# Down projections by seven products, added from PSUM to the residual, with the norm factor in the operands

## The chip, the cores and the metric

The kernel runs on one core of one Trainium2 chip. Its time is the device time of one execution in microseconds: 2298.66 us, the median of three runs (2298.14 to 2299.22).

## The reference

Two macaron layers over 528 tokens (512 plus 16 meta tokens) of width 1024. Each layer is a half-weighted SwiGLU, a mixer (gated linear attention and grouped-query attention, merged by sigmoid gates) and a second half-weighted SwiGLU. Each has an RMS norm ahead, and one stands at the end.

```python
def rmsnorm(x, g):
    y = xf * lax.rsqrt(jnp.mean(xf * xf, axis=-1, keepdims=True) + EPS)
    return (y * g.astype(jnp.float32)).astype(x.dtype)

def swiglu(x, w_gate, w_up, w_down):
    return (jax.nn.silu(x @ w_gate) * (x @ w_up)) @ w_down
...
        h = h + 0.5 * swiglu(rmsnorm(h, norm_gains[l, 0]),
                             ffn_w_gate[l, 0], ffn_w_up[l, 0], ffn_w_down[l, 0])
        h = h + mixer(rmsnorm(h, norm_gains[l, 1]), ...)
        h = h + 0.5 * swiglu(rmsnorm(h, norm_gains[l, 2]), ...)
```

The width of gate and up is 2816, 22 tiles of 128. Everything is float32.

## The kernel before

Activations lie with features on partitions and tokens along the free dimension: the residual `hall` is 8 chunks of 128 features by 528 tokens, and a token half is 264 columns (256 once the meta tokens have been dropped, in the last FFN). A float32 product is made from three matmuls: each operand is split into a rounded high part (`S.copy`, ScalarE, L222 for weights) and the rest (`V.tensor_tensor` subtract, VectorE, L227), and high x high, high x low and low x high are summed in PSUM.

Gate and up run by Strassen's scheme in Winograd's form. Two chunks of input features and two tiles of output features, with two token halves, make 2 x 2 blocks, and seven products stand for eight. `product_of_pair` (L489 to L530, matmuls at L502) does one product of one pair of output tiles: 24 matmuls of 264 columns. Products 1, 6, 7 and 4 add up in one PSUM tile X; snapshots of it on the way are copied out (`snapshot`, L505). Products 1, 2 and 4 use a plain block of weights; 7, 6, 5 and 3 use sums of blocks, which `sums` (L180) has made by DMA: a negated copy on ScalarE (L173), then DMAs that add while they write, issued from GpSimd's queue (L178). `pair` (L422) makes the seven activation blocks of two chunks.

Down runs plainly: `down` (L544) takes 22 hidden tiles to 8 output tiles, with the accumulations of three groups (4, 4 and 3 pairs) added to the residual (`add_to_h`, L471). The norm factor (one number per token) is not in the operands: it is multiplied in after the matmuls, by `scaled` (L467), on gate, on up, on down's output and on the mixer's projections, so that matmuls can start on a chunk before the mean over all chunks is known. `rs` (L458) makes the mean with an all-1/1024 matmul (L388), then Ln, Exp(-0.5) and a Newton step.

The order of weights is a list (`weight_plan`), written by `ffn_steps`. `Weights.use` keeps four blocks of 128 x 1024 made ahead (`AHEAD_MADE`) and six fetched; there are 3 raw buffers, 4 high, 4 low, and 3 and 2 for sums. Plain loads go through SP's queue (L168, L203), adding ones through GpSimd's, a few constants through ScalarE's. Each engine runs its instructions in one fixed order; the tile framework makes that order from the program's order, its priorities and its own estimate of times, and blocks marked `high_priority` come earlier. In the mixer, 12 of a layer's low parts are made by DMA (`by_dma`, L223).

## Time and profile before

| what | us |
|---|---|
| median of three runs | 2298.66 |
| span of the profiled execution, first to last instruction | 2289.1 |
| median less span: what lies around it (the page gives no other time of its own execution) | 9.6 |
| TensorE, matmuls busy | 2225.1 (97%) |
| VectorE busy | 1491.3 (65%) |
| ScalarE busy | 1214.4 (53%) |
| GpSimd busy | 195.1 (9%) |
| matmuls | 16548 |
| DMA, mean | 143 GB/s, 327.79 MB |

Rows of engines give busy time and share of the span. Matmuls are pipelined, so a mean of a group (285 ns at L502) is the latency of one and not its pace; the pace is a stretch of the chain divided by its count. The four FFNs lie at about 8 to 390, 806 to 1163, 1170 to 1536 and 1929 to 2272 us, the mixers between the first and second and the third and fourth.

### The profile page before, as it was taken

The numbers are of one execution on the slowest core, as the hardware profiler recorded it, in microseconds if no ns is written. First come the engines' busy times: TensorE is split into PE (matmuls) and PEld (weight loads), VectorE is DVE, ScalarE is ACT, GpSimd is POOL, SyncE is SP. The second block draws the span as 40 slices with busy tenths as digits, with TensorE's granted clock in tenths as the row PEclk, the third lists the DMA queues.
The fourth block names the chain that finished last, engine by engine and source line by source line (L and its number), as shares of the span: only waits on it lengthen the run. The fifth ranks groups of instructions, "written<-read, shape, count | busy, mean of one in ns | idle before, by whom it ended". The sixth has DMA issues, their size and how long they took to land.

```text
span 2289.1 us, 39919 instructions
## 1 busy us (share of the span) xinstructions
PE 2225.1 (97%) x16548; PEld 2108.4 (92%) x16548; DVE 1491.3 (65%) x2355; ACT 1214.4 (53%) x1785; POOL 195.1 (9%) x218
## 2 busy tenths in 40 slices
PE   5999999999999999999989999999999999999997
PEld 5999999989999999999989999998788888989896
DVE  6656567476775676565676565674768667756566
ACT  7536355344786564453565353553448946636452
POOL 1111010010000010101011110100000001101010
PEclk9999999999999999999989999999999999999999
DMA  8858562211325485766667585632113356859661
GB/s 225 236 150 224 142 175 93 74 57 56 84 56 157 117 214 153 189 180 173 181 141 202 151 219 146 170 98 74 56 65 93 74 156 152 223 149 223 159 176 61
DMA packets 91869, 327.79 MB, mean 143 GB/s; under 512 B 10214, under 2 KB 12646, under 8 KB 91688
## 3 DMA queue, kind: packets, MB, share of 16 engines
q1 hardware_dynamic: 61136, 218.26, 28.7%
q0 software_dynamic: 28800, 104.87, 25.6%
q8 instruction: 130, 2.13, 0.4%
q10 hardware_dynamic: 1752, 2.11, 0.3%
q14 instruction: 51, 0.42, 0.1%
HBM read 264.38 MB, written 2.10 MB: 116 GB/s over the span
## 4 chain that ended last, share of the span: by engine, by line
PE 89%; DVE 5%; DMA 2%; ACT 2%; issue 1%; SPq 0%; DVEq 0%; POOL 0%; ACTq 0%
PE ss L502 36%; PE ss L382 27%; PE mm L382 14%; PE sm L382 3%; PE sm L861 1%; PE sm L878 1%; DVE wlo L227 1%; PE sm L879 1%; PE ss L836 1%; DMA w<-win 1%; PE ss L837 1%; PE ss L388 1%; DMA s<-win 1%; PE ss L718 1%; DMA w<-s 1%
## 5 line engine op out<-in xcount | busy, mean ns | idle before, releaser
L502 PE MATMUL ss<-xc,whi 128*128 128x264 f32 (+1 forms) x4928 | 902.3, 285 | 26.5 <-ACT snap L508 9.7
L502 PEld LDWEIGHTS ss<-xc,whi 128*128 128x128 f32 x4928 | 766.8, 189 | 29.3 <-ACT snap L508 10.3
L502 PE MATMUL ss<-xc,wlo 128*128 128x264 f32 (+1 forms) x2464 | 702.1, 285 | 4.3 <-DVE wlo L227 4.3
L382 PE MATMUL ss<-g,whi 128*128 128x264 f32 (+2 forms) x2668 | 494.2, 301 | 0.0
L502 PEld LDWEIGHTS ss<-xc,wlo 128*128 128x128 f32 x2464 | 466.0, 189 | 5.3 <-DVE wlo L227 5.1
L382 PEld LDWEIGHTS ss<-g,whi 128*128 128x128 f32 x2668 | 388.6, 188 | 17.4
L382 PE MATMUL mm<-x,whi 128*128 128x264 f32 (+1 forms) x1712 | 383.5, 315 | 0.0
L222 ACT CAST whi<-w 128x1024 fp32r<-128x1024 f32 (+1 forms) x221 | 230.8, 1047 | 263.1 <-PE ss L382 118.7
L222 ACT CAST whi<-raw 128x1024 fp32r<-128x1024 f32 x190 | 199.3, 1049 | 299.5 <-PE mm L382 106.9
L227 DVE TENSOR_TENSOR wlo<-w,whi 128x1024 fp32r<-128x1024 f32 (+1 forms) x221 | 267.9, 1218 | 110.7 <-ACT whi L222 108.4
L382 PE MATMUL ss<-g,wlo 128*128 128x264 f32 (+2 forms) x1334 | 309.9, 301 | 0.0
L382 PEld LDWEIGHTS mm<-x,whi 128*128 128x128 f32 x1712 | 279.5, 189 | 18.8 <-issue 2.1
L382 PE MATMUL mm<-x,wlo 128*128 128x264 f32 (+1 forms) x856 | 267.2, 317 | 0.0
L227 DVE TENSOR_TENSOR wlo<-raw,whi 128x1024 fp32r<-128x1024 f32 x166 | 203.1, 1224 | 95.2 <-ACT whi L222 94.2
L382 PEld LDWEIGHTS ss<-g,wlo 128*128 128x128 f32 x1334 | 213.4, 188 | 8.7
L227 DVE TENSOR_TENSOR wlo<-s,whi 128x1024 fp32r<-128x1024 f32 x88 | 107.6, 1223 | 102.0 <-ACT whi L222 101.9
L222 ACT CAST whi<-s 128x1024 fp32r<-128x1024 f32 x88 | 92.4, 1050 | 153.6 <-PE ss L502 135.4
L382 PEld LDWEIGHTS mm<-x,wlo 128*128 128x128 f32 x856 | 160.4, 189 | 10.8 <-issue 2.2
L469 DVE SCALAR_TENSOR_TENSOR t<-ss,rs 128x528 f32<-128x528 f32 (+1 forms) x95 | 66.0, 700 | 127.8 <-PE ss L382 127.7
L173 ACT ACTIVATE s<-w 128x1024 f32<-128x1024 f32 x88 | 93.3, 1060 | 79.2 <-DMA w<-win 41.5
L178 POOL DMA_DIRECT2D s<-win x44 | 40.8, 927 | 497.0 <-ACT s L173 489.2
L508 ACT COPY snap<-ss 128x528 f32<-128x528 f32 (+1 forms) x132 | 77.2, 585 | 0.0
(235 smaller groups left out, 2660.3 us busy)
## 6 DMA issues: line engine op xcount, KB each, us to landing
w<-win SPq DMA_DIRECT2D x219, 512.0 KB, 4.7
raw<-wts SPq DMA_DIRECT2D x190, 512.0 KB, 3.4
s<-win POOLq DMA_DIRECT2D x44, 512.0 KB, 6.8
w<-s POOLq DMA_DIRECT2D x44, 512.0 KB, 5.5
w<-win POOLq DMA_DIRECT2D x44, 512.0 KB, 7.1
s<-w POOLq DMA_DIRECT2D x44, 512.0 KB, 7.4
wlo<-raw POOLq DMA_DIRECT2D x24, 512.0 KB, 4.4
h<-xt SPq DMA_DIRECT2D x3, 528.0 KB, 7.1
```

The lines of the kernel that those rows point to most:

```text
L173: self.nc.scalar.activation(t, w, AF.Copy, scale=-1.0)
L178: self.nc.gpsimd.dma_start(t, src, accum_op=ALU.add)
L222: nc.scalar.copy(hi[:, cs], w[:, cs])
L227: nc.vector.tensor_tensor(lo[:, cs], w[:, cs], hi[:, cs].bitcast(F32), ALU.subtract)
L382: TE.matmul(acc.half[i][:width], lhs, rhs[:, acc.spans[i]], start=first, stop=last)
L388: TE.matmul(a, weights, x[:, hs], start=True, stop=True)
L469: V.scalar_tensor_tensor(cut(dst[rows]), pv[rows], -0.5 * f, cut(rs[rows]), ALU.mult, ALU.mult)
L502: TE.matmul(acc[:, j], a[:, j, k], b[:, at], start=bool(begin and k == 0 and i == 0), stop=k == len(x) - 1 and i == 2, skip_group_check=no ...
L508: S.copy(st[name], acc)
L718: TE.matmul(ats[:n, hh, d * n : (d + 1) * n], prods[d][1][rows, bs], prods[d][0][rows, bs], start=True, stop=True)
L836: TE.matmul(s[:n, i, :HF], lhs, kh[:, hs], start=True, stop=False)
L837: TE.matmul(s[:n, i, :HF], lhs, kl[:, hs], start=False, stop=True)
```

## The change

The down projections are also done by seven products. Their 2 x 2 blocks are the two tiles of a pair of hidden features, two output chunks (m and m + 2, in each half `d` of four chunks) and the two token halves. An FFN is now a list of units: `("U", p)` for a pair of gate and up, `("D", g, d)` for one half of the output over group g; the groups are 3, 2, 3 and 3 pairs. Each product of a D unit has 6 matmuls of 264 columns per pair. Its PSUM tile is added to the residual as it is, by one VectorE operation (`of_half`), so X with products 1, 1+6, 1+6+7 and 1+6+7+4 goes to the places that need it. The hidden activations are made in seven blocks (`of_pair`); the half weight of the FFN goes into the gate. Down's weights come from a new array `wdn` in blocks of 768 or 512 columns, and pass through `sums` like gate's.

The norm factor is multiplied into the operands, by token halves: `square` and `square_chunk` sum squares per half as chunks are finished, `finish(i)` makes the mean and factor of half i and calls `operands(i)`. Products 1 and 2 need only half 0, 5 and 6 need half 1, and `rest` makes what 7, 3 and 4 need. An FFN therefore opens with products 1 and 2 of units 0 and 1 and product 2 of unit 2. Before it, w_out does its last three chunks by halves; the mixer does its first three projections by halves. Projections are copied out without a factor, `by_dma` is gone, and the constants of the mixer are loaded at the start of each mixer. At the end of the kernel each half of the residual is multiplied by its factor in two operations and stored in two DMAs.

```diff
-GROUPS = (4, 4, 3)
-HELD = 4
-PLACE = {p: i for i, p in enumerate("1256743")}
+GROUPS = (3, 2, 3, 3)
+NPAIR = FF // P // 2
+WIDEST = 256 * max(GROUPS)
+PLACE = {p: i for i, p in enumerate("1256734")}
 DIRECT = {"1": "11", "2": "12", "4": "22"}
+BLOCKS = ("11", "12", "21", "22")
...
+    def rest(q):
+        if q in ends:
+            a, b, n = q + 1, q + 2, GROUPS[units[q + 1][1]]
+            put((q, "7"))
+            put((a, "1"), part=1)
+            put((q, "4"), (q, "3"))
+            put((a, "2"), part=1)
+            put((a, "1"), part=2)
+            put((a, "2"), part=2)
+            if b + 1 < len(units):
+                put((a, "6"), (a, "5"), (a, "7"), (b, "1"), (a, "4"), (b, "2"), (a, "3"), (b, "6"), (b, "5"))
+                rest_of_half(b)
+            else:
+                put((a, "6"), (b, "1"), (a, "7"), (b, "2"), (a, "4"), (b, "6"))
+                put((a, "5"), part=tuple(range(n - 1)))
+                put((b, "7"))
+                put((a, "5"), part=(n - 1,))
+                put((b, "4"), (b, "5"), (a, "3"), (b, "3"))
+        else:
+            rest_of_half(q)
...
+    steps.append((((0, "1"), (0, "2")), 0))
+    put((1, "1"), (1, "2"), (2, "2"))
+    steps.append((((0, "6"), (0, "5")), 0))
+    early.append((2, "2"))
+    put((1, "6"), (0, "7"), (1, "5"), (0, "4"), (1, "7"), (0, "3"))
+    put((2, "1"), (1, "4"), (1, "3"), (2, "6"), (2, "5"))
+    rest(2)
+    return units, steps
...
+    def sums(self, f, unit, product, w):
         got = self.summed
+        late = unit not in EARLY_SECOND
+        if product == "2" and not late:
+            return
         if product == "1":
...
+            s3 = self.negative(f, unit, "s3", w)
+            self.add(s3, self.dram(f, unit, "21"))
+            s2 = self.block(f, unit, "22", self.short, "wsb")
             self.add(s2, s3)
...
+            got[f, unit, "7"], got[f, unit, "6"] = s3, s2
+            if not late:
+                w = self.block(f, unit, "12")
+        if product == "2" or not late:
+            s1 = self.block(f, unit, "21", self.short, "wsb")
+            self.add(s1, self.dram(f, unit, "22"))
+            s4 = self.negative(f, unit, "s4", w)
+            self.add(s4, got[f, unit, "6"])
+            got[f, unit, "5"], got[f, unit, "3"] = s1, s4
     def fetch(self, upto):
...
             w = self.raws.pop(s, None)
...
+        def square(self, chunks, i, last=False):
+            s = self.sum_tile()
+            src = hall[:, chunks[0] : chunks[1] + 1 : chunks[1] - chunks[0], half(i)]
+            with tc.high_priority():
+                if i in self.started:
+                    sq = v2(slot("n"))
+                    S.activation(sq, src, AF.Square)
+                    if last:
+                        self.tail = [sq[:, 0], sq[:, 1]]
+                    else:
+                        V.tensor_tensor(s[:, i], s[:, i], sq, ALU.add)
+                else:
+                    self.started.add(i)
+                    S.activation(s[:, i], src, AF.Square)
+            for c in chunks:
+                self.scale(c, i)
...
+        def finish(self, i, ms):
             w = live[0] // 2
...
+            s = self.sums[:, i]
             with tc.high_priority():
...
+                V.tensor_tensor(s[:, 0], s[:, 0], s[:, 1], ALU.add)
+                terms = [s[:, 0]] + self.tail
+                for k, t in enumerate(terms):
+                    TE.matmul(ms[:, :w], o1024, t, start=k == 0, stop=k == len(terms) - 1)
+                with after(table("natural_log_exp_and_others")) if i == 0 else nullcontext():
+                    u = slot("n")[:, :w]
+                    rsqrt(ms[:, :w], self.rs[:, half(i)], u)
+            self.operands(i)
+        def operands(self, i):
+            w, rs = live[0] // 2, self.rs[:, half(i)]
+            two = rs.unsqueeze(1).broadcast_to([P, 2, w])
+            if self.kind == "x":
+                for c in range(KC):
+                    if i == 0:
+                        self.x[c] = [slot("x", F32R), slot("x", F32R)]
+                    hi, lo = [t[:, half(i)] for t in self.x[c]]
+                    v = self.low[c // 2][:, c % 2, i]
+                    V.tensor_tensor(v, v, rs, ALU.mult)
+                    parts(hi, lo, v)
+            elif self.kind == "xc":
+                for j in range(KC // 2):
+                    v = self.low[j][:, i]
+                    if i == 0:
+                        self.x[j] = [seven("xc", F32R) for _ in range(2)]
+                    hi, lo = self.x[j]
+                    V.tensor_tensor(v, v, two, ALU.mult)
+                    if i == 0:
+                        parts(hi[:, 0:2], lo[:, 0:2], v)
+                    else:
+                        low, t = self.low[j][:, 0], seven("hc")
+                        V.tensor_tensor(t[:, 0], v[:, 0], low[:, 0], ALU.subtract)
+                        V.scalar_tensor_tensor(t[:, 1], v[:, 1], -1.0, t[:, 0], ALU.mult, ALU.subtract)
+                        parts(hi[:, 2:4], lo[:, 2:4], t[:, 0:2])
+                        V.tensor_tensor(low[:, 0], low[:, 1], t[:, 1], ALU.subtract)
+            else:
+                for c in (0, KC // 2):
+                    cs = half(i)
+                    t = hall[:, c : c + KC // 2, cs]
+                    V.tensor_tensor(t, t, rs.unsqueeze(1).broadcast_to([P, KC // 2, w]), ALU.mult)
+                    (S if c else nc.sync).dma_start(out[:, c : c + KC // 2, cs], t)
+        def rest(self):
+            for j, (hi, lo) in self.x.items():
+                low, v = self.low[j][:, 0], self.low[j][:, 1]
+                V.tensor_tensor(v[:, 0], v[:, 0], v[:, 1], ALU.add)
+                parts(hi[:, 4:6], lo[:, 4:6], v)
+                parts(hi[:, 6], lo[:, 6], low[:, 0])
...
+            for k in work[0][-1]:
+                for acc, whi, wlo, ops, product, nk, _ in work:
+                    xh, xl = ops[k]
+                    at = PLACE[product]
+                    begin = product in begins
+                    for j in range(2):
+                        for i, (a, b) in enumerate(((whi, xh), (whi, xl), (wlo, xh))):
+                            TE.matmul(acc[:, j], a[:, j, k], b[:, at], start=begin and k == 0 and i == 0,
+                                      stop=k == nk - 1 and i == 2, skip_group_check=not begin)
+            for (u, product), t in zip(which, work):
+                if t[-1][-1] == t[-2] - 1:
+                    (of_pair if UNITS[u][0] == "U" else of_half)(u, product)
...
+        def of_pair(u, product):
+            st, p = state[u], UNITS[u][1]
+            X, Y, Z = [st[b][:, :, :w] if b in st else None for b in "XYZ"]
+            if "c1" not in st:
+                st["c1"] = plane("c1")
             if product == "1":
...
+                st["c2"] = plane("c2")
+                hid[p] = [seven("hc", F32R) for _ in range(2)]
+            c1, c2 = st["c1"], st.get("c2")
+            last = p in ends
+            if product in "12":
+                both = "both" in st
+                st["both"] = True
+                with tc.high_priority():
+                    if both:
+                        V.tensor_tensor(c1[:, :, 0], c1[:, :, 0], X if product == "1" else Y, ALU.add)
+                    else:
+                        S.copy(c1[:, :, 0], X if product == "1" else Y)
+                if both and u > 1:
+                    gate(c1[:, 0, 0], c1[:, 0, 0], c1[:, 1, 0], 0.5)
+                    if last:
+                        hi, lo = hid[p]
+                        parts(hi[:, 0], lo[:, 0], c1[:, 0, 0])
+                return
+            hi, lo = hid[p]
+            t = c2.rearrange("p j q c -> p (j q) c")
+            if product == "6":
+                with tc.high_priority():
+                    S.copy(c1[:, :, 1], X)
             elif product == "7":
...
+                with tc.high_priority():
+                    S.copy(c2[:, :, 1], X)
+                    V.tensor_tensor(c2[:, :, 1], c2[:, :, 1], Z, ALU.add)
+                if u < 2:
+                    gate(c1[:, 0, 0], c1[:, 0, 0], c1[:, 1, 0], 0.5)
+                gate(t[:, 3], t[:, 1], t[:, 3], -0.5)
+                V.tensor_tensor(t[:, 1], c1[:, 0, 0], t[:, 3], ALU.subtract)
             elif product == "4":
...
+                with tc.high_priority():
+                    act(t[:, 0], X[:, 0], AF.Silu)
+                    V.scalar_tensor_tensor(c1[:, 1, 0], t[:, 0], 0.5, X[:, 1], ALU.mult, ALU.mult)
+                if last:
+                    parts(hi[:, 1], lo[:, 1], c1[:, 1, 0])
             elif product == "3":
...
+                with tc.high_priority():
+                    V.tensor_tensor(c1[:, :, 1], c1[:, :, 1], Z, ALU.add)
+                gate(c1[:, 0, 1], c1[:, 0, 1], c1[:, 1, 1], 0.5)
+                V.tensor_tensor(t[:, 1], t[:, 1], c1[:, 0, 1], ALU.subtract)
+                if last:
+                    parts(hi[:, 3], lo[:, 3], t[:, 1])
+                V.tensor_tensor(t[:, 0], c1[:, 0, 1], c1[:, 0, 0], ALU.subtract)
+                V.tensor_tensor(t[:, 2], c1[:, 0, 1], t[:, 3], ALU.add)
+                V.tensor_tensor(c1[:, 1, 1], c1[:, 1, 0], t[:, 1], ALU.subtract)
+                if last:
+                    parts(hi[:, 2], lo[:, 2], t[:, 0])
+                    parts(hi[:, 4:6], lo[:, 4:6], t[:, 2:4])
+                else:
+                    parts(hi[:, 0:2], lo[:, 0:2], c1[:, :, 0])
+                    parts(hi[:, 2:6], lo[:, 2:6], t)
+                parts(hi[:, 6], lo[:, 6], c1[:, 1, 1])
+        def gate(dst, g, u, f):
+            act(g, g, AF.Silu)
+            V.scalar_tensor_tensor(dst, g, f, u, ALU.mult, ALU.mult)
+        places = {"1": [(0, 0)], "2": [(0, 0)], "6": [(0, 1)], "3": [(0, 1)], "7": [(1, 1)], "5": [(1, 1)], "4": [(1, 0)]}
+        done = {"2": (0, 0), "4": (1, 0), "3": (0, 1), "5": (1, 1)}
+        def of_half(u, product):
+            st, (_, g, d) = state[u], UNITS[u]
+            acc = st[bank[product]][:, :, :w]
+            for m, i in places[product]:
+                hv = hall[:, 4 * d + m : 4 * d + m + 3 : 2, half(i)]
+                with tc.high_priority():
+                    V.tensor_tensor(hv, hv, acc, ALU.add)
+            if g == len(GROUPS) - 1 and product in done:
+                m, i = done[product]
+                last = d == 1 and product in "43"
+                nxt.square((4 * d + m, 4 * d + m + 2), i, last)
+                if last:
+                    nxt.finish(i, pair(kind(len(UNITS) - 2 + i))[:, 0])
+        last_u = max(i for i, (which, _) in enumerate(STEPS) if any(UNITS[u][0] == "U" for u, _ in which))
+        for i, (which, part) in enumerate(STEPS):
...
+        for m in range(KC - 3):
+            add(m, product("w_out", Acc(kinds[m]), y, KC), None)
+            nxt.square_chunk(m)
+        late = range(KC - 3, KC)
+        accs = {m: Acc(kinds[m], cut=True) for m in late}
+        w = {m: [W.next("w_out") for _ in range(KC)] for m in late}
+        for i in range(2):
+            for m in late:
+                products([accs[m]], [(w[m], y)], (i,), KC)
+                add(m, accs[m], i)
+                nxt.square_chunk(m, i, m == KC - 1)
+            nxt.finish(i, pair()[:, 0] if i == 0 else sm())
```

596 lines of the change are left out of this document (279 added, 317 removed).

## The prediction

> **What bounds the kernel now.** I read the page first (busy time, then the chain of work that ended last), then who the matmul engine waited for, then the chain in order of time and windows by stage.
>
> ```profile
> span 2289.1 us, 39919 instructions
> PE 2225.1 (97%) x16548; PEld 2108.4 (92%) x16548; DVE 1491.3 (65%) x2355; ACT 1214.4 (53%) x1785; POOL 195.1 (9%) x218
> PE 89%; DVE 5%; DMA 2%; ACT 2%; issue 1%; SPq 0%; DVEq 0%; POOL 0%; ACTq 0%
> PE ss L502 36%; PE ss L382 27%; PE mm L382 14%; PE sm L382 3%; PE sm L861 1%; PE sm L878 1%; DVE wlo L227 1%; PE sm L879 1%; PE ss L836 1%; DMA w<-win 1%; PE ss L837 1%; PE ss L388 1%; DMA s<-win 1%; PE ss L718 1%; DMA w<-s 1%
> ```
>
> TensorE is the bound: 89% of the chain is matmuls, 36% the seven products of gate and up (L502), 27% at L382 into the wide accumulators, which is mostly the down projection. The span stands 9.56 us below the 2298.66 us median of the three runs; the page gives no other time for its execution, so I build a new span and add 9.56. Where TensorE is not running, it waits here:
>
> ```profile
> PE ss L502 <- ACT snap L508: 9.7, 1, 9.7
> PE ss L502 <- ACT whi L222: 9.2, 2, 7.8
> PE ss L502 <- ACT xc L433: 7.3, 1, 7.3
> PE ss L388 <- DVE t L420: 5.4, 3, 2.7
> ```
>
> ```profile
> 0.00:95.00 95.00, 71.52 (x529) 69.25 (x530) 64.48 (x97) 63.96 (x93) 14.37 (x20) 0.95 0.90 240
> 40.00:95.00 55.00, 54.88 (x450) 54.67 (x450) 35.27 (x43) 32.56 (x41) 9.47 (x11) 1.00 0.94 240
> 806.00:811.00 5.00, 3.60 (x27) 3.28 (x26) 4.81 (x9) 4.02 (x8) 0.00 (x0) 1.00 0.61 186
> 830.00:1163.00 333.00, 332.82 (x2735) 332.60 (x2733) 212.50 (x275) 166.90 (x206) 35.02 (x40) 1.00 0.71 179
> 1163.00:1180.00 17.00, 7.16 (x32) 6.46 (x33) 14.27 (x28) 10.98 (x21) 1.76 (x2) 0.60 0.54 120
> ```
>
> In the windows (columns: length, busy time of PE, PEld, DVE, ACT and POOL, granted clock, DMA share, GB/s) the FFN itself, 830 to 1163, has no idle matmul time. Loss sits at three kinds of place: the start, the joint of two FFNs (1163 to 1180: 17 us for 32 matmuls, at a granted clock of 0.60), and the tail. The joint of mixer and FFN (806 to 811) loses about 1.4 us.
>
> **The change, part by part.** *Fewer matmuls.* Down has 22 row tiles times 8 output tiles times 3 terms times 2 halves of 264 columns, 1056 matmuls per FFN. The seven products have, over four groups with 11 pairs, 2 output halves x 7 x 11 x 6 = 924.
>
> ```profile
> 938.00 73.19 PE ss L502 x600
> ...
> 1028.69 37.65 PE ss L382 x312
> ...
> 1169.06 0.34 DVE t L442
> ...
> 1171.60 0.62 DVE xc L434
> ...
> 2055.54 70.93 PE ss L502 x600
> ...
> 2143.28 36.18 PE ss L382 x156
> ```
>
> A product matmul costs 73.19/600 = 0.122 us, a down matmul 37.65/312 = 0.1207. 1056 x 0.1207 - 924 x 0.122 = 14.7 us, three times. In the last FFN a down matmul has 512 columns, 36.18/156 = 0.232, and a product 70.93/600 = 0.118: 528 x 0.232 - 924 x 0.118 = 13.4. Together **-57.5 us**. An FFN is then (1848 + 924) x 0.122 = 338 us of matmuls.
>
> *Operands, on VectorE and ScalarE.* Down's weights become 7 blocks where there were 4, and the hidden activations 7 blocks per pair where there were 4.
>
> ```profile
> L227 DVE TENSOR_TENSOR wlo<-w,whi 128x1024 fp32r<-128x1024 f32 x51 | 62.0, 1223 | 21.2 <-ACT whi L222 20.5
> L222 ACT CAST whi<-w 128x1024 fp32r<-128x1024 f32 x51 | 53.6, 1051 | 63.1 <-PE ss L382 31.5 <-PE ss L502 29.6 <-ACT g L370 1.7
> L515 DVE TENSOR_TENSOR c<-snap,ss 128x528 f32<-128x528 f32 x10 | 7.0, 699 | 1.6 <-PE ss L502 1.6
> L541 DVE TENSOR_TENSOR c<-c 128x264 f32<-128x264 f32 x11 | 4.7, 427 | 0.0
> ```
>
> VectorE per FFN: weights 77 slabs, and down's 7 x 5632 = 39,424 columns (38.5 slabs), at 1.223: 141 us. A pair: three PSUM additions of 528 columns at 0.70, nine operations of 264 at 0.43, low parts of 7 x 264 columns, some 2.4: 8.4, times 11 is 92. The residual: 8 units x 7 additions x 0.70 = 39. The norm's operands: per pair of chunks five of 0.70 and five of 0.43, times 4 is 23. Sum 295 of 338 us, 87%, against 212.5 of 333 now. Back to back, operations start 0.62 and 0.34 apart in the chain, so 78% is the other bound. ScalarE's casts grow by (38.5 - 22) x 1.051 = 17 us per FFN and stay below VectorE. On average both are hidden by matmuls; in bursts not, in two places. (1) After the last pair of a group. Unit a's product 6 adds to the bank of its product 1, and only six matmuls (0.73 us) stand between; it must wait for the 0.70 us residual addition, which queues behind up to 1.2 us of a weight's low part: 0 to 1.2 us. From the pair's product 3 to the end of unit a's product 7 there are 78 matmuls, 9.5 us; VectorE has in them, by spacing, six operations of 0.62 (two of the pair, four residual additions), eight of 0.34 and four low parts of 768 columns at 0.87: 9.9 us (in the group of two 8.8 for 6.6), which the blocks made four ahead absorb in part. I take 0.9 us per group, 16 groups: **+14**, bounds 0 and 48 (3 us each). (2) The first 13 products of an FFN (38 us) need the 23 us of norm operands, 14 low parts (17) and about 6 of two pairs: 46 busy, 40 by spacing. I take 3 us at three joints, **+9** (0 to 24); at the kernel's start DMA hides it.
>
> *Transfers.* Down's blocks now need what gate's need: five plain loads and four accumulating ones per block set, and the accumulating issues go to POOL's queue, 76 per FFN for 44.
>
> ```profile
> q0 software_dynamic: 6336, 23.07, 37.8%
> q1 hardware_dynamic: 10933, 39.81, 33.5%
> w<-win SPq DMA_DIRECT2D x54, 512.0 KB, 4.9
> raw<-wts SPq DMA_DIRECT2D x22, 512.0 KB, 4.0
> w<-s POOLq DMA_DIRECT2D x11, 512.0 KB, 5.5
> s<-win POOLq DMA_DIRECT2D x11, 512.0 KB, 5.7
> ```
>
> This is 811 to 1163, one FFN (352 us). 44 accumulating transfers took 37.8% of it, 3.02 us of all engines each; 76 plain ones 33.5%, 1.55 each. A set of one unit's blocks costs 4 x 3.02 + 5 x 1.55 = 19.8 us. The new FFN has 11 sets and 8 smaller ones worth 5.5: 16.5 x 19.8 = 327 us for 338 us of matmuls, a share of **0.97** where the whole FFN now has 0.71. Speaking for it: from 40 to 95 us the share was 0.94 with 450 matmuls in 55 us, full pace. POOL issues cost 0.9 us each by its 35.02 us for 40, so 76 fit easily. The chain of a sum (cast, negate, add from memory, add between tiles) takes about 1.2 + 0.9 + 5.7 + 5.5 us for 512 KB. A group of three has 384 KB: in proportion 4.3 + 4.1, some 11.5 with the rest, against 126 matmuls (15.4 us) from unit a's product 2, which frees the slot for unit b's first block, to b's product 6. A group of two has 2.9 + 2.8, some 8, against 10.2. Covered if latency does not rise; I take **+6** (0 to 40).
>
> The Trainium skill, "DMA: Bandwidth & Descriptors", section "Anatomy of one DMA", speaks against the proportion: about 2.0 us of a transfer are fixed, whatever its size. By that, an estimate, the two additions take 4.8 + 4.6 and 3.9 + 3.8 us, and the group of two would stall some 2 us more each time, 8 us over the kernel. The present trace has no accumulating block below 512 KB and cannot decide.
>
> *The norm factor.* Operands now wait for the mean, so each joint has a chain. The tail of the kernel shows its links:
>
> ```profile
> 2267.98 4.52 PE ss L382 x37
> ...
> 2277.39 0.34 DVE t L1021
> ```
>
> ```profile
> 809.99 1.13 PE L388 MATMUL ss<-t,const 128*128 128x264 f32 x4 [1.40 <-DVE t L420]
> ```
>
> From the last down matmul to the finished factor of a half: 2272.5 to 2277.7, 5.2 us. The new chain drops two VectorE operations (0.9), adds one or two mean terms of 0.28 to 0.56 us, then a 0.70 us product and a cast (0.6): 6.5 us. Cover for the first half: at an FFN's end three products of 18 matmuls, 6.6 us; at w_out's end three chunks of half 1, 72 x 0.1207 = 8.7 us. Cover for the second half: before an FFN five products that need only half 0, 14.6 us; before the mixer 8.7 us. So a stall of about 1.5 us at each FFN-to-mixer joint where there is none now: **+3** (0 to 16); mixer to FFN unchanged; between the FFNs 13 us of loss (17 us less 32 matmuls) become 3: **-10** (-13 to 0). If a cover fails, the price is the chain itself, 6.5 us, and the clock. The mean has 2 or 3 terms per half where it had one: up to 3.4 us for 1.13, in five places, in TensorE's own stream: **+8**. *Tail*: 16.6 us from 2272.5 to the end lose one scaling, one addition and a chain of half chunks: **-4.5** (-8 to 0).
>
> *Start.* 529 matmuls in 95 us are 30.5 us late, all before 40 us. The lateness is the sum chain behind product 1:
>
> ```profile
> 2.61 6.28 DMA h<-xt
> ...
> 14.08 9.05 DMA s<-win
> ```
>
> ```profile
> 7.75 0.81 PE L502 MATMUL ss<-xc,whi 128*128 128x264 f32 x2 [7.75 <-ACT whi L222]
> ```
>
> The new order puts five products without sums (14.6 us) first, but its first matmul waits for half of x (I take 6 us, as later chunks land at 2.61 + 6.28 = 8.9), squares and the 6.5 us chain: say 14 us where it is 7.75 now. 14 + 1.5 of slow clock + 14.6 = 30 us; by then a sum begun at 14 us as now has its first addition (14.08 + 9.05 = 23) and its second (5.5 us). Lateness 20 instead of 30.5: **-10** (-16 to +6).
>
> *Mixer.* Scalings by the factor become copies (equal counts); 24 low parts go from DMA to VectorE (24 x 1.22, beside 5.8 us of matmuls each), and 16 gate scalings per layer go. 0, between -8 and +8.
>
> Sum: -57.5 + 14 + 9 + 6 + 3 - 10 + 8 - 4.5 - 10 = -42. Span 2247, time **2257 us**, own range 2238 to 2280.
>
> **The rivals.** (A) *All covers hold*: without the 14, 9, 6 and 3 the time is 2225 us. For it: no wait at all inside today's FFN. Against: VectorE goes from 64% to 78-87%. (B) *VectorE paces the turns*: 3 us per group in place of 0.9, 48 for 14: 2291 us. For it: 9.9 us of work in 9.5; against: four blocks made ahead. (C) *DMA becomes the bound*, the slower side. It decides when the queues, with three plain and five sum buffers, hold less than the needed 0.97: at 0.90 an FFN takes 327/0.90 = 363 us, 25 more, four times 100, with 29 of my stalls inside it: 2328 us, slower. The break-even is at about 71/4 = 18 us, a share of 0.92. For it: today's best long stretch is 0.94; against: its own prices, by the rows below of the same stretch, 5.88 MB being 11.2 blocks and 6.39 MB 12.2, are (57.6% x 55)/11.2 = 2.83 and (31.1% x 55)/12.2 = 1.40 us: 18.3 per set, a need of only 0.89.
>
> ```profile
> q0 software_dynamic: 1612, 5.88, 57.6%
> q1 hardware_dynamic: 1767, 6.39, 31.1%
> ```
>
> (D) *The clock falls at the turns.* At 1163 to 1180 a 7.3 us wait left a clock of 0.60; 0.4 of 7.16 us is 2.9 us per event. Sixteen events are 46 us: 2303 us. Against: the 1.4 us wait at 806 left 1.00. The Trainium skill, "TensorE: Matmul & The Clock Gate", section "A second HAM failure mode: psum-queue depth-cycling", says short idles between bank turns can do this; the trace shows it only after a long wait.
>
> **How the numbers follow.** Forecast 0.50, A 0.20, B 0.10, C 0.15, D 0.05. The range 2222 to 2300 leaves out most of C, half of D and a little of A, about 0.2. No change means within 0.2%, 2294 to 2303, about what a measurement can tell: a third of B, half of D and a little of C, 0.07. Faster is the forecast, A and two thirds of B, 0.77; slower 0.16.
>
> **What would show it.** Right: matmuls at 264 columns 4 x 132 fewer in the FFNs; FFN windows of 340 to 352 us at clock 1.00; the first product running by 16 us; waits of TensorE of 1 to 2 us on residual additions and operands at group ends, none above 3 us. DMA share in the FFNs near 0.9. Wrong: FFN windows of 360 us with waits on casts behind transfers (C), VectorE above 90% there (B), granted clock under 0.97 inside an FFN (D), or a joint with an idle of 6 us or more.

## The result, and the profile after

The changed kernel takes 2422.7 us (median; 2413.6 to 2426.0) where the kernel before took 2298.4: a ratio of 1.054, interval 1.0515 to 1.0567. It is 124 us slower, and 166 us above the forecast. The profiled execution took 2423.4 us with a span of 2421.6. First its page: span, busy time of the engines, the DMA queues with packets, MB and share of 16 engines, and the group of weight casts.

```profile
span 2421.6 us, 41861 instructions
PE 2247.2 (93%) x16724; PEld 2134.0 (88%) x16724; DVE 1663.2 (69%) x2794; ACT 1381.5 (57%) x2247; POOL 280.7 (12%) x316
q0 software_dynamic: 43776, 138.43, 32.2%
q1 hardware_dynamic: 72272, 230.75, 28.3%
L274 ACT CAST whi<-w_U 128x1024 fp32r<-128x1024 f32 (+1 forms) x221 | 228.4, 1041 | 208.9 <-DMA w_U<-win 85.8
```

TensorE is busy for 22 us more than before, though the change was to save it 57 us, and idle for 174 us instead of 64. The last row is the new thing: before, the casts of a weight's high part waited for TensorE to free their tiles; now transfers end most of this group's waits (85.8 us a transfer from memory, 80.2 the link into the second sum). Who TensorE waited for (total, times, longest):

```profile
PE ss L632 <- ACT whi L274: 64.8, 28, 7.8
PE ss L632 <- DVE wlo L275: 20.0, 26, 4.2
PE ss L632 <- ACT c L676: 15.1, 11, 3.6
PE ss L539 <- DVE sums L536: 12.5, 5, 6.6
PE ss L632 <- DVE h L719: 6.2, 15, 1.1
```

The windows by stage (length, busy time of PE, PEld, DVE, ACT and POOL, clock, DMA share, GB/s) are the start, FFN 0, mixer 0, FFNs 1 and 2, mixer 1, FFN 3 and the tail; behind them FFN 0, mixer 0, FFNs 1 and 2, mixer 1 and FFN 3 of the kernel before, between the same marks:

```profile
0.00:21.30 21.30, 5.41 (x12) 3.76 (x13) 8.52 (x19) 14.44 (x28) 2.08 (x6) 1.00 0.83 260
21.30:413.80 392.50, 356.95 (x2780) 350.85 (x2778) 276.42 (x410) 230.20 (x342) 64.77 (x74) 0.96 0.83 201
413.80:842.40 428.60, 418.94 (x3268) 398.16 (x3267) 277.05 (x589) 231.73 (x454) 11.23 (x9) 0.99 0.23 71
842.40:1625.30 782.90, 718.49 (x5568) 704.30 (x5566) 556.24 (x830) 456.39 (x678) 128.62 (x147) 0.96 0.82 198
1625.30:2030.00 404.70, 396.26 (x2319) 334.18 (x2318) 267.44 (x530) 223.08 (x409) 11.78 (x9) 0.99 0.25 75
2030.00:2408.90 378.90, 349.34 (x2783) 341.64 (x2782) 271.26 (x413) 221.96 (x334) 62.19 (x71) 0.96 0.79 193
2408.90:2421.60 12.70, 1.83 (x9) 1.14 (x7) 6.23 (x9) 3.66 (x8) 0.00 (x0) 0.81 0.47 165
```

```profile
7.80:392.80 385.00, 369.28 (x2973) 366.90 (x2974) 250.64 (x328) 198.53 (x253) 38.69 (x44) 0.99 0.68 179
392.80:806.50 413.70, 406.82 (x3196) 386.60 (x3195) 269.82 (x579) 237.06 (x442) 22.01 (x21) 1.00 0.32 87
806.50:1538.00 731.50, 720.00 (x5850) 716.96 (x5849) 473.00 (x613) 371.64 (x464) 72.54 (x83) 0.99 0.68 171
1538.00:1929.00 391.00, 385.12 (x2136) 318.44 (x2136) 260.86 (x519) 228.00 (x399) 22.38 (x21) 1.00 0.33 91
1929.00:2272.40 343.40, 342.06 (x2397) 318.84 (x2395) 223.41 (x290) 171.19 (x212) 34.12 (x39) 1.00 0.67 169
```

The four FFNs take 1554 us for some 1341 us of matmuls at full pace, at a clock of 0.96 and a DMA share of 0.79 to 0.83. They hold the loss.

The four sums of a unit are, in the code, s3 (product 7), s2 (product 6), s1 (product 5) and s4 (product 3). To s3 and s1 a transfer adds a block from memory; s2 adds s3, and s4 adds s2: these two are the links. The text below and most of the recorded expectations call s1, s2 and s4 the first, second and fourth sum; where an expectation speaks of the link from the first sum into the second, it means s3.

One stall in full, the longest wait for a cast, at the end of FFN 2, from the timeline (start, length, engine, line, operation, and in brackets the idle time before it and what ended that):

```profile
1593.48 0.87 POOL L224 DMA_DIRECT2D s_D<-w_D  x1 [7.06 <-ACT s_D L219]
...
1602.71 0.33 SPq L214 DMA_DIRECT2D w_D<-wdn  x1
...
1606.53 0.87 POOL L224 DMA_DIRECT2D w_D<-wdn  x1 [12.19 <-DMA w_D<-wdn]
...
1611.64 0.83 ACT L274 CAST whi<-w_D 128x768 fp32r<-128x768 f32 x1 [11.21 <-DMA w_D<-wdn]
```

```profile
1604.00:1613.00 9.00, 1.22 (x9) 1.00 (x7) 0.50 (x1) 1.36 (x2) 0.87 (x1) 0.71 0.54 138
1612.00:1625.00 13.00, 11.68 (x73) 11.24 (x74) 9.27 (x12) 9.96 (x19) 0.00 (x0) 0.77 0.21 62
```

Read it from the end. TensorE stands from 1604.7 to 1612.5 for the weights of one product (the 7.8 us above). Their cast waits for the first sum's accumulating transfer, issued at 1606.53. That waited on GpSimd's queue for the plain load into the same tile, issued only at 1602.71 although SyncE had nothing else to do: the load needs one of the two buffers `wsb`, and the one that comes free still holds the second sum, which the fourth sum's transfer of 1593.48 reads. That transfer landed after 9.2 us, at about 1602.6, beside loads and constants for the next mixer; the median of its kind is 5.7. So three transfers and a cast stand in one line, 19 us long, with the DMA engines only 54% busy while TensorE stands; then the clock is at 0.77 for the next 13 us. In the whole kernel SyncE's queue stands like this 40 times behind a fourth sum of gate/up and 27 times behind one of down. The last row is the same wait in the kernel before (L168 is the load there), 36 times, where it cost nothing, as the first experiment shows: the chain is old, its length and the missing slack are new.

```profile
SPq L214 <- DMA s_U<-w_U: 423.5, 40, 16.3
...
SPq L214 <- DMA s_D<-w_D: 96.1, 27, 11.1
```

```profile
SPq L168 <- DMA s<-w: 198.5, 36, 13.1
```

### The profile page after: what moved, and what is told of

The parts are those of the page before. It is cut to its first block, busy times and chain, and to the rows that moved or that the text cites. A ratio compares the mean times of both kernels' runs of the same rounds, so it can differ in the third digit from the quotient of the medians.

```text
span 2421.6 us, 41861 instructions
## 1 busy us (share of the span) xinstructions
PE 2247.2 (93%) x16724; PEld 2134.0 (88%) x16724; DVE 1663.2 (69%) x2794; ACT 1381.5 (57%) x2247; POOL 280.7 (12%) x316
## 5 line engine op out<-in xcount | busy, mean ns | idle before, releaser
L632 PE MATMUL ss<-xc,whi 128*128 128x264 f32 (+1 forms) x4928 | 935.4, 291 | 67.8 <-ACT whi L274 32.5
L632 PEld LDWEIGHTS ss<-xc,whi 128*128 128x128 f32 x4928 | 787.4, 194 | 80.3 <-ACT whi L274 44.7
L632 PE MATMUL ss<-xc,wlo 128*128 128x264 f32 (+1 forms) x2464 | 713.2, 290 | 17.5 <-DVE wlo L275 17.3
L632 PE MATMUL ss<-hc,whi 128*128 128x264 f32 (+1 forms) x2464 | 466.4, 290 | 38.5 <-ACT whi L274 32.3
L632 PEld LDWEIGHTS ss<-xc,wlo 128*128 128x128 f32 x2464 | 478.2, 194 | 22.0 <-DVE wlo L275 22.0
L275 DVE TENSOR_TENSOR wlo<-w_U,whi 128x1024 fp32r<-128x1024 f32 (+1 forms) x221 | 267.5, 1218 | 239.5 <-ACT whi L274 239.2
L632 PEld LDWEIGHTS ss<-hc,whi 128*128 128x128 f32 x2464 | 388.9, 192 | 46.4 <-ACT whi L274 34.8
L427 PE MATMUL mm<-x,whi 128*128 128x264 f32 (+2 forms) x1728 | 385.1, 314 | 2.0 <-ACT x L411 2.0
L632 PE MATMUL ss<-hc,wlo 128*128 128x264 f32 (+1 forms) x1232 | 351.1, 287 | 2.7 <-DVE wlo L275 2.7
L274 ACT CAST whi<-w_U 128x1024 fp32r<-128x1024 f32 (+1 forms) x221 | 228.4, 1041 | 208.9 <-DMA w_U<-win 85.8
L427 PE MATMUL mm<-x,wlo 128*128 128x264 f32 (+2 forms) x864 | 269.6, 315 | 0.0
L632 PEld LDWEIGHTS ss<-hc,wlo 128*128 128x128 f32 x1232 | 234.8, 192 | 4.3 <-DVE wlo L275 4.2
L275 DVE TENSOR_TENSOR wlo<-w_D,whi 128x768 fp32r<-128x768 f32 (+1 forms) x160 | 140.4, 889 | 98.8 <-ACT whi L274 97.9
L427 PEld LDWEIGHTS mm<-x,wlo 128*128 128x128 f32 x864 | 163.1, 190 | 10.2 <-issue 2.2
L719 DVE TENSOR_TENSOR h<-h,ss 128x528 f32<-128x528 f32 (+1 forms) x224 | 155.1, 696 | 22.6 <-PE ss L632 21.6
## 6 DMA issues: line engine op xcount, KB each, us to landing
w_D<-wdn SPq DMA_DIRECT2D x40, 256.0 KB, 4.0
```

The costliest lines, as they stand in the source:

```text
L274: nc.scalar.copy(hi[:, cs], w[:, cs])
L275: nc.vector.tensor_tensor(lo[:, cs], w[:, cs], hi[:, cs].bitcast(F32), ALU.subtract)
L427: TE.matmul(a.half[i][: lhs.shape[-1]], lhs, rhs[:, a.spans[i]], start=k == 0 and j == 0, stop=k == nk - 1 and j == 2)
L632: TE.matmul(acc[:, j], a[:, j, k], b[:, at], start=begin and k == 0 and i == 0, stop=k == nk - 1 and i == 2, skip_group_check=not begin)
L719: V.tensor_tensor(hv, hv, acc, ALU.add)
```

## The experiments

Each result is one execution with its profile, beside one of the kernel before on the same chip (2289 to 2297 us there). Two cautions hold for all. The changed kernel was not run on those chips; where the kernel before takes 2289 in place of 2298, a difference from 2422.7 may be up to 9 us too large (the 151 below would be 142). And the order of instructions on ScalarE and VectorE is made by the tile framework's planner, and follows its costs, so an edit also moves instructions: by the traces, about 100 of the 2968 on ScalarE are out of the old sequence in `no_link`, about 700 in `more_bufs`. TensorE's order is unchanged in `no_link`.

### All sums without their transfers, here and in the kernel before

```diff
-            self.add(s3, self.dram(f, unit, "21"))
...
-            self.add(s2, s3)
...
-            self.add(s1, self.dram(f, unit, "22"))
...
-            self.add(s4, got[f, unit, "6"])
```

> The four accumulating transfers of every unit are left out, so the four weight sums hold only their first operand (a negated cast or a plain load); the output isn't the reference's, every matmul, cast, copy and vector sum stays. If the sums made by transfers (their bytes or their chain) cost the 125 us, the time falls to 2235 to 2280. If the turns of the groups on VectorE and in the PSUM banks cost it, it stays at 2390 to 2420. If the norm factor in the operands and the late start cost it, it stays above 2380.

> The kernel before without the accumulating transfers of its gate/up units (sums incomplete, output not the reference's). If they were covered there, the time is within 0.3% of 2298; if they cost something there already, 2270 to 2288.

Measured: 2271.5 and 2289.6 us. The accumulating transfers cost the changed kernel 151 us (142 by the chips' own kernel before), and those of gate and up cost the kernel before nothing: 2289.6 against 2289.3 on the same chip. Windows of the three FFN stretches without them:

```profile
21.60:379.60 358.00, 346.78 (x2779) 342.76 (x2778) 279.07 (x410) 231.71 (x342) 0.00 (x0) 0.99 0.37 125
805.90:1512.80 706.90, 693.38 (x5567) 685.56 (x5566) 560.64 (x830) 458.92 (x678) 0.00 (x0) 0.99 0.38 125
1917.90:2257.10 339.20, 334.33 (x2784) 330.84 (x2782) 273.18 (x413) 224.66 (x334) 0.00 (x0) 1.00 0.36 121
```

1404 us in place of 1554. Of the 150 between them, 100 are idle time of TensorE (130 against 30) and 50 are busy time (1425 against 1374): the same matmuls at a lower clock (0.96 against 0.99 to 1.00). Mixers, start and tail hardly differ.

### The down units' transfers alone, and the gate/up units' alone

```diff
-            self.add(s3, self.dram(f, unit, "21"))
+            if unit[0] == "U":
+                self.add(s3, self.dram(f, unit, "21"))
```

(and so for the other three; `"D"` in the second run)

> Only the eight down units of an FFN lose their four accumulating transfers (their sums are incomplete, so is the output); the eleven gate/up units keep theirs. If the down units' transfers fill the gaps in which the chain of the gate/up units caught up in the kernel before, most of the loss goes: 2260 to 2320. If the gate/up units are late by themselves, 2350 to 2400.

> The reverse of the run without the down units' adds: the eleven gate/up units lose their four accumulating transfers (sums incomplete, output not the reference's), the eight down units keep them. All adds cost 151 us, and leaving out the down units' gave 65 back. If the two kinds add up, this gives 86 back: about 2337. If each kind is late only beside the other (traffic that sums up, one queue), it gives much more: 2275 to 2300. If the down units' own chain is late since their products are shorter (18 matmuls against 24, 12 in the small group), most of the loss stays: 2350 to 2400.

Measured: 2357.3 without the down units', 2314.6 without the gate/up units'. Over the run without any (2271.5) the gate/up units' transfers alone cost 86 us, the down units' alone 43, and both together 142 to 151. The second lies between two of its expectations: the kinds mostly add up, at most 22 us come from their being together, and each is late by itself. For the gate/up units that is new, since the same transfers cost the kernel before nothing: there down's plain tiles stood between the groups, and here shorter products with loads of their own do, which I take to be the reason. It was not tried by itself, nor apart from the other thing that changed there, the order of the products and with it of the loads.

### The links, the data, the place in time

```diff
-            self.add(s2, s3)
+            self.add(s2, self.dram(f, unit, "21"))
...
-            self.add(s4, got[f, unit, "6"])
+            self.add(s4, self.dram(f, unit, "22"))
```

> As many accumulating transfers of the same size, each still into a tile, but all of them now read DRAM: the second sum adds block 21 and not the first sum, the fourth adds block 22 and not the second sum. Left out of the computation: the two links from one sum to the next (output not the reference's). If the chain of landings (each link waits for the one before on the one queue of GpSimd) holds the casts up, 2260 to 2330. If the amount of data is what costs, or the price of an accumulating transfer itself, 2390 to 2430.

```diff
-        self.nc.gpsimd.dma_start(t, src, accum_op=ALU.add)
+        n = t.shape[-1] // 2
+        self.nc.gpsimd.dma_start(t[:, :n], src[:, :n], accum_op=ALU.add)
```

> Every accumulating transfer is made on the first half of its columns only (256 KB for a gate/up unit in place of 512; the other half of each sum is left out, output not the reference's): as many transfers, links, queue entries and waits, half the data. If the amount of data costs, most of the 151 us between the kernel after and the one without accumulating transfers goes: 2280 to 2320. If the number of serial steps costs, at a length of each that the size sets only in part, 2340 to 2390.

```diff
             self.got[s] = (hi, lo)
+            if load in self.later:
+                self.add(w, self.later.pop(load))
```

> Every accumulating transfer keeps its size and its queue and reads DRAM, but it is issued into its tile only after that tile has been cast (the sums are missing from the matmuls, output not the reference's): the traffic is that of the changed kernel, and no cast waits for a sum. If the casts' waits for the sums are what costs (a chain that lands late, with transfers else healthy), 2275 to 2310. If the traffic costs by making the plain loads of the blocks late too, it stays between 2340 and 2400.

Measured: 2383.4 without links, 2343.3 with half of the data, 2660.8 with the transfers behind the casts. Neither end of the first expectation: the links are worth 39 us (30 by the chip's own kernel before) and not the whole. This run also takes away the hold of the stall shown above, since no transfer reads the second sum's tile any more; SyncE's waits behind a fourth sum (423.5 and 96.1 us) are gone from its list, and the larger part of the loss stays. Half of the data is worth 79, just inside the range of the serial steps (shorter transfers also land sooner, so this run does not separate the two). The third missed by 260 us, and shows a cost that I had not thought of: a tile stays taken until the transfer into it has landed, and the next unit waits for the tile, ScalarE's negations (the rows below) and SyncE's loads alike.

```profile
ACT s_U L220 <- DMA s_D<-wdn: 194.5, 34, 10.9
ACT s_D L220 <- DMA s_U<-win: 187.0, 47, 6.5
```

### Who issues, and who adds

```diff
-            self.nc.sync.dma_start(w[:, a[0] : a[-1] + 1], self.dram(f, unit, name)[:, a[0] : a[-1] + 1])
+            (self.nc.gpsimd if tag == "wsb" else self.nc.sync).dma_start(w[:, a[0] : a[-1] + 1], self.dram(f, unit, name)[:, a[0] : a[-1] + 1])
```

> The plain loads into the two buffers of the second and the first sum are issued from GpSimd's queue in place of SyncE's; the same data, everything computed. SyncE's queue then no longer stands behind a buffer that the fourth sum's transfer still reads (423.5 us of waits, 40 of them, in the changed kernel), and the direct blocks behind it come in time. If that standing queue is what makes the casts late: 2340 to 2390. If the traffic makes them late whatever the queue: 2400 to 2440; if GpSimd's queue, with two loads more a unit, becomes the later one: above 2440.

```diff
+    def sum(self, t, src):
...
+        self.nc.gpsimd.tensor_tensor(t, t, src, ALU.add)
...
-            self.add(s2, s3)
+            self.sum(s2, s3)
...
-            self.add(s4, got[f, unit, "6"])
+            self.sum(s4, got[f, unit, "6"])
```

> The two links of each unit (the first sum into the second, the second into the fourth) are made by GpSimd's own tensor additions instead of accumulating transfers; everything is computed. It takes away half of the accumulating traffic, and a queue step. Estimate from the additions that GpSimd makes in the mixers (528 columns in 1780 ns): 3.5 us for 1024 columns, 118 us an FFN on an engine that is idle there. If traffic and chain are the cause: 2290 to 2330, with DMA shares of 0.65 to 0.75 in the FFNs. If GpSimd's additions are as late as the transfers were, since they wait for the same landings in the same order: 2370 to 2420.

```diff
-                s4 = self.negative(f, unit, "s4", w)
-                self.add(s4, got[f, unit, "6"])
...
+        self.nc.vector.tensor_tensor(s4, w, self.held.pop((f, unit)), ALU.subtract)
```

> The fourth sum is one subtraction on VectorE (second sum minus block 12), placed behind the cast of the second sum, in place of ScalarE's negation and an accumulating transfer, for all units but the first three of each FFN (those keep the transfer); everything is computed. It takes away a link, a ScalarE pass (1.06 us) and about 3.0 of the 19.5 us of transfers a unit, and adds 1.22 us to VectorE (a cast's subtraction of that size), 78 us in all. If traffic and chain are the cause: 2340 to 2385 (the half of the adds' data gave 79 us back, this takes a quarter of it, and the link). If VectorE then holds up the turns: 2400 to 2440.

> Both edits: the fourth sum on VectorE, and the plain loads of the two sum buffers from GpSimd's queue. With the fourth sum's transfer gone from GpSimd's queue there is room for the loads. If queue and traffic are separate causes, the gains add up: 2300 to 2350. If both relieve the same wait: no more than the better of the two, 2340 to 2385.

Measured: 2449.4, 2453.4, 2498.3 and 2478.5 us. The first is the third of its cases: the loads no longer make SyncE's queue stand behind a fourth sum, but on GpSimd's queue they stand among the additions, and TensorE waits longer for casts (81.2 us for 64.8). The other three missed, all on the slow side. GpSimd's additions slowed VectorE, which is busy for 1872.1 us in place of 1663.2: the subtraction of a cast, 1223 ns in the changed kernel, took 1412:

```profile
L279 DVE TENSOR_TENSOR wlo<-w_U,whi 128x1024 fp32r<-128x1024 f32 x219 | 307.4, 1412 | 104.0 <-ACT whi L278 103.7
```

(The Trainium skill, "SBUF — State Buffer", section "Who interferes with whom", has VectorE operations with two SBUF inputs contend with GpSimd's reads; this row agrees.) On VectorE the fourth sum stood waiting for the second sum's landing, and the residual additions (the second row, 6.2 us in the changed kernel) came late behind it:

```profile
DVE s_U L256 <- DMA w_U<-s_U: 135.6, 20, 9.7
```

```profile
PE ss L645 <- DVE h L732: 67.9, 26, 7.5
```

My reading is that the late sum is the same and each edit only chose which in-order engine stands still for it; for the additions on GpSimd it is only argued.

### Traffic without waits

High and low parts of the FFN operands share a tile in these four runs, to make room.

```diff
     def add(self, t, src):
-        self.nc.gpsimd.dma_start(t, src, accum_op=ALU.add)
+        self.nd += 1
+        self.nc.gpsimd.dma_start(self.dummies[self.nd % 6][:, : t.shape[-1]], src, accum_op=ALU.add)
```

> All 76 accumulating transfers of an FFN are made, from DRAM, at their old places in GpSimd's queue and with their sizes, but into six tiles that nothing reads: the traffic is whole, and no cast, no buffer of a sum and no other transfer waits for one. (The sums are missing from the matmuls; and to find room for the six tiles, high and low parts of the FFN operands share a tile, which changes values and no instruction count. Output not the reference's.) If the traffic by itself makes the plain loads late: 2340 to 2400. If only the waits for the sums cost (links, buffers, landings): 2266 to 2295, as without any adds.

2397.3 us, but not for the expected reason: nothing held the transfers back, and they ran far ahead. Two halves of FFN 0:

```profile
25.50:220.00 194.50, 164.93 (x1221) 160.28 (x1222) 130.30 (x202) 105.70 (x161) 56.32 (x65) 0.93 1.06 250
220.00:418.50 198.50, 195.17 (x1558) 193.38 (x1557) 148.06 (x210) 125.74 (x182) 4.58 (x6) 0.98 0.44 141
```

At a share of 1.06 (a rough share can pass 1) TensorE does 1221 matmuls in 194 us, at 0.44 it does 1558 in as long. A plain load of 512 KB into a unit's tiles lands 10.3 us after its issue in the first half (median of 24) and 3.3 in the second (of 26): so many transfers at once do make the plain loads late. So each transfer was paced by a small operation on the tile that it would have changed:

```diff
+        d = self.dummies[self.nd % 6]
+        self.nc.gpsimd.tensor_tensor(d[:, :1], t[:, :1], t[:, :1], ALU.add)
+        self.nc.gpsimd.dma_start(self.dummies[self.nd % 6][:, : t.shape[-1]], src, accum_op=ALU.add)
```

> As the run with adds into six tiles that nothing reads, but each add now stands behind a one-column GpSimd operation on the tile that it would have added to, so that it starts no sooner than in the changed kernel: whole traffic, spread as there, and no cast, buffer or transfer waits for its landing. (Sums missing, high and low parts of the FFN operands in one tile; output not the reference's.) If traffic alone makes the plain loads late: 2340 to 2400. If the waits for the sums are what costs: 2270 to 2300.

```diff
-                        self.x[j] = [seven("xc", F32R) for _ in range(2)]
+                        self.x[j] = [seven("xc", F32R)] * 2
```

> The changed kernel with nothing but the shared tile for high and low parts of the FFN operands (values differ, output not the reference's), the common ground of the three runs that needed its room. If sharing costs nothing: 2410 to 2430, and those three can be read against the changed kernel. If it changes the order of the work or the waits: away from that, and they are read against this one.

> No accumulating transfer at all (sums incomplete), and the shared tile for high and low parts of the FFN operands; output not the reference's. It is the floor for the run with paced adds that nothing reads (2313.4) and the run with the shared tile alone (2401.1). If the shared tile costs nothing here: 2262 to 2280; then the spread traffic costs 35 to 50 us and the waits for the sums 88. If the shared tile itself saves time: 2240 to 2260, and the traffic costs more than that.

Measured: 2313.4 paced, between its two expectations; 2401.1 with the shared tile alone, below its first; 2273.7 with the shared tile and no transfers, in its first. The first two ran on one chip, the third on one whose kernel before differs by 1 us. This is the division of the loss on common ground: **88 us are waits for sums** (2401.1 to 2313.4) and **40 us are the traffic** (2313.4 to 2273.7). The paced run in FFN 0 and its waits for casts:

```profile
21.20:386.30 365.10, 349.52 (x2780) 344.75 (x2778) 277.87 (x410) 231.20 (x342) 94.55 (x148) 0.98 0.85 214
```

```profile
PE ss L636 <- ACT whi L278: 11.4, 11, 2.2
```

All transfers made, at a share of 0.85, and TensorE waits 11 us for casts in place of 50 with the shared tile alone. The plain loads of 512 KB even land later than in the changed kernel (median 6.5 us for 5.2), so late plain loads are not what the 88 are. (Its transfers all read DRAM, so the links are part of the 88. A transfer that stands for a link waits for its tile and no longer for the sum before it, so it can start sooner than in the changed kernel, other than the expectation says; that too is a wait for a sum.) The shared tile alone moved the time by 21 us: I take that as the size of what the planner's order does, and don't explain it. An effect of that size can also lie in the 88 and in the 40.

### More buffers, and copies on VectorE

```diff
-        pools = open_pools("left", wsa=3, wsb=2, hc=2 * max(GROUPS))
+        pools = open_pools("left", wsa=6, wsb=4, hc=2 * max(GROUPS))
```

> The changed kernel with six and four buffers for the sums in place of three and two, all transfers and links as they are. (The room comes from letting high and low parts of the FFN operands share a tile; output not the reference's.) If the loads and negations wait for a buffer that a transfer still holds, and this makes the sums late: 2290 to 2350. If the links' length against the time from a unit's first cast to its third makes them late, or the traffic does: 2390 to 2430.

```diff
-                    S.copy(c1[:, :, 1], X)
+                    V.tensor_copy(c1[:, :, 1], X)
```

(and so for the copies of products 7 and 1 or 2)

> The three copies of a pair's sums from PSUM to SBUF are made by VectorE (about 700 ns each by its additions of that shape) in place of ScalarE (590 ns); everything is computed. If copies that stand on ScalarE behind a cast which waits for a transfer are what holds the PSUM tiles, and with them TensorE: 2380 to 2405 (the waits for such copies are 25 us). If the casts themselves are what TensorE lacks: 2415 to 2435. VectorE gets 71 us more in all: above 2435 if it sets the pace of the turns.

Measured: 2464.1 with six and four buffers, 63 above the run with the shared tile alone, and 2415.8 with the copies on VectorE, not told from the changed kernel. Who ScalarE and TensorE waited for with more buffers:

```profile
ACT s_D L219 <- DMA w_D<-wdn: 183.5, 53, 8.9
ACT s_U L219 <- DMA w_U<-win: 135.0, 49, 7.1
```

```profile
PE ss L632 <- ACT c L676: 99.5, 25, 8.1
```

The buffers did what they were for: SyncE's wait behind the fourth sums of gate/up falls from 422.5 us with the shared tile alone to 256.0, and TensorE's wait for casts from 49.9 to 14.8. But ScalarE now stands at a block's negation until the block has landed, 318 us in these two rows, and TensorE waits 99.5 us for the copies of its sums behind it, in place of 15.9. I take the planner's order for the cause, since a tile is now free early; it was not tried. So this run does not show what buffers alone would give; that stays open. The copies run fits its second case, that in the changed kernel TensorE lacks the casts themselves and the copies behind them are a small part.

### The norm factor

```diff
-                    V.tensor_tensor(v, v, two, ALU.mult)
+                    V.tensor_tensor(v, v, eps.unsqueeze(1).broadcast_to([P, 2, w]), ALU.mult)
```

> The kernel without accumulating transfers (2271.5), and the FFN operands are multiplied by a constant column instead of the norm factor (output not the reference's), so that nothing of an FFN waits for the mean and its root; the mean's matmuls and the root stay. If the norm factor in the operands costs its 12 us at the start and some at each joint: 2245 to 2258. If the joints hide it, only the start is saved: 2258 to 2264.

Measured: 2266.1 us, 5.4 below the run that it is made from, or 9 by the two chips' kernels before (2292.7 and 2289.3). That is less than the first expectation, and less than the second or just in it: the FFN operands' wait for the factor costs 5 to 9 us in all, and the start gained nothing; the first product still comes at 21.5 us:

```profile
21.46 1.01 PE L628 MATMUL ss<-xc,whi 128*128 128x264 f32 x2
```

## Why the prediction was wrong

**Fewer matmuls, -57.5.** Right: the groups at L632 count 11,088 matmuls, 2772 an FFN. Without transfers the gain shows: TensorE is busy for 1374 us in the FFN windows, 57 less than in those of the kernel before (1431), of which some 11 are other matmuls that ran inside the old windows.

**Transfers, +6 (0 to 40).** This is the step that failed; it measured 142 to 151. The price per transfer was right: 0.83 of 392.5 us is 326 us of DMA work in FFN 0, where I had 327. What failed is the cover ("covered if latency does not rise"), in three ways.

First, I costed the chains of down only and gave the gate/up units' transfers no term, since today's FFN has no wait; alone they cost 86 us in the new order, down's alone 43.

Second, the chain that I costed had two additions and ended at the second sum. The real one goes on: the fourth sum's transfer holds the second sum's tile, the next load waits for that tile, and the next first sum for the load, on two in-order queues, as at 1593 to 1612. The run without links gave 30 to 39 us for this part; the rest of the 88 us, by what the paced run takes away, is casts and tiles that wait for the transfer into their own tile, and no run divides it further.

Third, I let latency shrink with the size and stay as it was in a kernel at a share of 0.71. Median us from issue to landing after, from memory and from tile, by size:

```profile
s_U<-win POOLq DMA_DIRECT2D x44, 512.0 KB, 7.4
w_U<-s_U POOLq DMA_DIRECT2D x44, 512.0 KB, 5.5
s_D<-wdn POOLq DMA_DIRECT2D x24, 384.0 KB, 7.5
w_D<-s_D POOLq DMA_DIRECT2D x24, 384.0 KB, 4.5
s_D<-wdn POOLq DMA_DIRECT2D x8, 256.0 KB, 6.5
w_D<-s_D POOLq DMA_DIRECT2D x8, 256.0 KB, 3.7
```

For the two additions of a group of two I had 2.9 + 2.8 us and a chain of 8 against a cover of 10.2; they took 6.5 + 3.7, which with the 2.3 us of cast and negation makes a chain of 12.5, over the cover. In the group of three 7.5 + 4.5 for 4.3 + 4.1 makes it 15.1 against 15.4. So this chain alone, at its measured latencies, would stall only the groups of two, some 2 us each time; it does not make the loss. The rule of the Trainium skill that I weighed there ("DMA: Bandwidth & Descriptors", "Anatomy of one DMA") gave, by my estimate, 4.6 and 3.8 us for the additions from a tile; the rows say 4.5 and 3.7, so it was nearer than the proportion. For those from memory it gave 4.8 and 3.9, too low for 7.5 and 6.5 here. The excess goes with the traffic: in the run where only the down units had such transfers, the same two took 4.9 and 4.0 us.

**Rival C**, DMA as the bound, was the right family with a wrong number. Its formula, 327 us over the share that the queues hold, gives 394 us at the measured 0.83, and 392.5 was measured; as a share is DMA work over time, that says no more than that the price was right. The cheaper price that I held against C, a need of 0.89, was not (19.6 us a set by the page's shares after, not 18.3). I had put the share at 0.90 at worst, from a stretch of 55 us at 0.94, and took it for a bound of the DMA engines. But with the same data, and nothing that waits for it, the FFN takes 365 us at a share of 0.85: 310 us of DMA work, so the price falls too and the share hardly rises. The share does not set the time; the larger part of the loss is the waits for the sums, the 40 us of traffic are C's own. I gave C 0.15; the case's own row of a need of 0.97 deserved more.

**Rival D**, the clock: its sign came true (0.96 in the FFNs; "under 0.97" was my mark), not its cause. Without transfers, with all turns as they are, it is 0.99 to 1.00; after the one wait for a cast followed above it was 0.77. The lower clock takes 50 of the 150 us in the FFNs: the waits are paid twice.

**Turns +14, and rival B.** Right in kind: 15 waits on residual additions, 6.2 us in all, 1.1 at most. VectorE's 276 us in FFN 0 are near my 295, and it did not pace the FFNs: without transfers it has the same work (279 us) in a shorter FFN, TensorE waits only 9.6 us for low parts in all four FFNs, and it idles 30 us in all FFNs together, where turns, operands and the FFN joint were to take about 26.

**The start, -10.** Wrong. I had the first product at 14 us, since it needs half 0 only. In the profile of the changed kernel:

```profile
9.34 1.22 PE L539 MATMUL ss<-sums,o 128*128 128x264 f32 x2 [9.34 <-DMA o<-const]
...
18.88 1.25 PE L539 MATMUL ss<-sums,o 128*128 128x264 f32 x2 [6.55 <-DVE sums L536]
19.91 1.97 PE L539 MATMUL ss<-n,o 128*128 128x264 f32 x4
21.31 1.01 PE L632 MATMUL ss<-xc,whi 128*128 128x264 f32 x2
```

The program calls `finish` for both halves ahead of the FFN, so TensorE's order has the mean of half 1 ahead of the first product, and that product waits for the whole of x; with a constant for the factor it starts no earlier.

**Joints, tail, mixer.** The tail is 3.9 us shorter (12.7 for 16.6; I had 4.5). The norm's cover held before the FFNs: 5 to 9 us in all. Before the mixers it was not tried. The mixers are 14.9 and 13.7 us longer between the marks; by the counts of the windows, 69 and 42 of their matmuls ran ahead of the mark before (2973 less 2904, 5850 less 5808), some 8 and 5 us. That leaves about 15 us for both, where I had some 9 (3 for the joints, most of the 8 for the mean terms, 0 for the mixer). The 6 or 7 us over that and the 7.3 us of the start are 14 of the 20 us between the run without transfers (2271.5) and my sum without their term (2251); by that chip's own kernel before the gap is some 30, and the rest stays open.

## What to carry to other kernels

Cost a transfer that others wait for as a chain with its buffers: follow every tile from its load to the landing of the last transfer that reads it, on each in-order queue, at the latency that it has under the traffic that the change brings. A need of 0.97 of the DMA engines is no margin: here the engines were busy for 0.83 of an FFN that took 392.5 us in place of 338, and with the same data, spread out and waited for by nobody, the kernel took 88 us less. A chain that was covered in one order of the work has to be costed again in the next. And read the program's order on each engine before crediting an early start to data that is ready early.

## What the runs showed that I had not expected

- One TensorE wait of 8 us was followed by 13 us at a granted clock of 0.77; in the FFNs as a whole a third of the loss is clock and not idle time.
- With GpSimd additions of up to 1024 columns beside them, VectorE's subtractions of that size were 15% longer on the mean (1412 for 1223 ns).
- Six free target tiles let GpSimd's queue run so far ahead that one half of FFN 0 had 65 of its transfers and the other 6, and the kernel lost nearly as much as with the waits.
- More tiles for the sums made the kernel 63 us slower: ScalarE then stood 318 us at negations for loads, and TensorE behind it.
